# Ring slots of split weights set further apart, a bonus tied behind later chunks, and more filler ahead of the last transposes

## The chip, the cores and the metric

One core of a Trainium2 chip runs one program. The metric is the device time of one execution in microseconds (us), lower is better. TensorE (PE) has a weight loader that works beside it (PEld in the rows); VectorE is DVE, ScalarE is ACT, GpSimd is POOL, and SyncE is SP. SP and POOL issue nearly all of the DMAs.

## The reference

One layer over x of 256 tokens by 2048, in float32: an FFN, two token mixers side by side (latent attention and an RWKV recurrence) that two gates join, cross-attention into 256 memory tokens, and a second FFN. Each has an RMSNorm ahead and behind. The change sits around the recurrence and what is done to its output:

```python
def step(state, inp):                       # 16 heads, state 64 x 64 each, 256 tokens
    r_t, w_t, k_t, v_t, a_t, b_t = inp
    sa = einsum('bhvk,bhk->bhv', state, a_t)
    state = state * w_t + sa[..., None] * b_t[:, :, None, :] + v_t[..., None] * k_t[:, :, None, :]
    return state, einsum('bhvk,bhk->bhv', state, r_t)
...
o = (o - mean) * rsqrt(var + LNX_EPS)       # group norm per head
o = o * lnx_w + lnx_b
bonus = sum(rh * kh * r_k) * vh
return ((o + bonus) * g) @ w_ob             # g = sigmoid(dg) @ w_g2
```

## The kernel before

**Weights.** Every large product is done in two halves of each weight. A tile of 128 x 1024 float32 weights arrives by an SP DMA in `wraw` (4 buffers); ACT casts it to `whi` (L204) and DVE subtracts to get the rest, `wlo` (L205). Both halves go to one of RING = 3 slots of two long tiles, `whi` and `wlo`; slot s starts at WT * s = 1024 s numbers, plus a small shift (STILL) where the weights are the stationary operand. `lin_ch` (L226, L229) keeps the weights stationary, `lin_tok` (L253 to L255) streams them, three matmuls of 512 columns for each step of k and token half.

**Order of the work.** A scheduler sets the order on each engine from priorities and from readiness. In the recurrence's stage PE's order is written by hand: `weave` runs `rwkv()`, and wherever that yields a number of microseconds it puts in so many steps of `fill()`, each counted as TOK_US = 0.68. In the stretch looked at here a step of filler is three matmuls of a gate's projection (`mm<-whi,hT`), and the filler is finite: what is used early is missing later.

**The recurrence** (`rw_chain`) goes over 8 chunks of 32 tokens, numbered c0 to c7 here. In each chunk PE does `po<-S` (L953, not in c0), three steps of filler, `pu` (L963), four steps, `pn` (L972, not in c7), the rest of `po` (L982), and the first part of the next chunk's `po` (L938), then three steps. Between them ACT copies `rhs`, ACT and DVE copy one half each of `pu` into `uv` (L966), DVE makes the new state S (L979, L980; L977 in c0), and ACT copies `po` to `o`, which POOL's queue writes to memory (`osc`, L992). `last_o` counts the chunks written.

**The output** of a token half t is made of `ab` and `z`. `rw_scale` loads two rows (`lnx`) and v (`ab`) by POOL's queue, scales v by the bonus (L1010), adds a row (L1011), multiplies by the gate `pg`, a PE product (L1013, then L1014, L1015). `rw_group_norm` loads `osc` as `ov`, normalizes it on DVE with a power on POOL (L1033) and joins it with `ab` (L1035, L1036). `transposed` turns `ov` by PE (L333) into `z`, which the product with w_ob needs. For t = 0, `ab` is made early in the chain and the transposes of z[0] stand after c6; for t = 1, `ab` is tied behind the `osc` write of c6 (the argument `behind`), the group norm stands after c7, and the transposes of z[1] after 16.0 us of filler.

`after(a, b)` ties a behind b: in order alone where both are on one engine, with a semaphore otherwise.

Of the kernel before, what the change touches and what calls it, by code (L numbers as in the profile page):

```python
# [10 lines left out]
F32 = mybir.dt.float32  # L11
F32R = mybir.dt.float32r
# [6 lines left out]
P = 128  # L19
D = 2048  # L20
T = 256
# [5 lines left out]
WT = 1024  # L27
RING = 3
STILL = (64, 32)
SKEW = 4  # L30
# [49 lines left out]
class Layer:  # L80
    def __init__(self, ctx, tc, a):
# [30 lines left out]
        self.hold = []  # L112
        self.whi = self.hi_pool.tile([P, RING * WT + STILL[0]], F32R, tag="whi", name="whi")
        self.pad(self.hi_pool, 512 - 4 * STILL[0])
        self.wlo = self.lo_pool.tile([P, RING * WT + STILL[1]], F32R, tag="wlo", name="wlo")
        self.X = self.hpool.tile([P, NT, D], F32, tag="big", name="X")

    def pad(self, pool, n):

        pool.tile([P, n // 4], F32, tag="pad", name="pad")  # L120

# [63 lines left out]
    def weights(self, w, nk, c0, n, feed=None, still=False):  # L185
# [3 lines left out]
        for k in range(0, nk, kt):  # L189
            m = min(kt, nk - k)  # L190
            raw = self.wraw.tile([P, WT], F32, tag="wraw", name="wraw")
            a, b = (WT * self.turn + x for x in (STILL if still else (0, 0)))
            self.turn = (self.turn + 1) % RING
# [246 lines left out]
    def ffn(self, normed, wg, wu, wd, post):  # L440
        nc = self.nc
        h, _, row, *feed = normed
        with self.tc.tile_pool(name="hid", bufs=1) as hid:
            mh = hid.tile([P, KF, T], F32R, tag="mh", name="mh")
            ml = hid.tile([P, KF, T], F32R, tag="ml", name="ml")
            for c0 in range(0, DFF, 256):
# [3 lines left out]
                def ev_gate(j, ps):  # L450
                    sg = hid.tile([P, T], F32, tag="sg", name="sg", bufs=4)
                    nc.vector.tensor_mul(sg, ps, row())
                    nc.scalar.activation(out=sg, in_=sg, func=AF.Silu)
                    nc.vector.tensor_mul(sg, sg, row())
                    gate[j] = sg
# [88 lines left out]
    def mla_latents(self, mp, pool, normed):  # L544
        nc, w_in = self.nc, self.a["w_in"]
        h, r, _ = normed
        self.pad(pool, 224)
        self.cqh = pool.tile([P, 4, T], F32R, name="cqh")
# [192 lines left out]
    def rw_alloc(self, pool):  # L741
        self.pad(pool, 32)
        self.ar = pool.tile([P, 2, NC, GP, 64], F32, tag="ar", name="ar")
        self.bk = pool.tile([P, 2, NC, GP, 64], F32, tag="bk", name="bk")
        self.wc = pool.tile([P, NC, PAIRS], F32, tag="wc", name="wc")
        self.osc = self.dram.tile([T, 1024], F32, name="osc")
# [178 lines left out]
    def rw_chain(self, pool, G):  # L925
# [18 lines left out]
        po = from_values(0, uvs[0])  # L944
        yield 58.0
        for c in range(NC):
# [21 lines left out]
            if c < NC - 1:  # L968
# [7 lines left out]
                if S is None:  # L976
                    nc.vector.tensor_mul(Sn, pn, w)  # L977
                else:
                    nc.vector.tensor_add(Sn, S, pn)  # L979
                    nc.vector.tensor_mul(Sn, Sn, w)  # L980
            for p, h in heads:
# [4 lines left out]
            if c < NC - 1:  # L986
                S = Sn
                po = from_values(c + 1, uvs[c + 1])
            o = pool.tile([P, PAIRS, 64], F32, tag="o", name="o", bufs=2)
            nc.scalar.copy(out=o, in_=done)  # L990
# [7 lines left out]
    def rw_scale(self, pool, t, h, bon, behind):  # L998
# [10 lines left out]
        v = ab[:, 1, :].rearrange("p (h v) -> p h v", v=64)  # L1009
        nc.vector.tensor_mul(v, v, bon[:, t, h * H : (h + 1) * H].unsqueeze(2).broadcast_to([P, H, 64]))  # L1010
        nc.vector.tensor_add(ab[:, 1, :], ab[:, 1, :], rows[:, 1, :])  # L1011
        pg = self.psm.tile([P, 512], F32, tag="mm", name="pg")
        self.after(nc.tensor.matmul(pg, self.sg[:, ts], self.wg2[:, cs], start=True, stop=True), behind)  # L1013
        nc.vector.tensor_mul(ab[:, 0, :], rows[:, 0, :], pg)  # L1014
        nc.vector.tensor_mul(ab[:, 1, :], ab[:, 1, :], pg)  # L1015
# [51 lines left out]
    def mix(self, normed, xsp, stop=None):  # L1067
# [3 lines left out]
        with tc.tile_pool(name="mixp", bufs=1) as mp:  # L1071
            self.cst = mp.tile([P, NCST], F32, name="cst")
            nc.scalar.dma_start(out=self.cst, in_=a["cst"])
            self.pad(mp, 256)
            with tc.tile_pool(name="mla", bufs=1) as pool:
                self.rope_tables(pool)
                self.rw_columns(mp)
                self.mla_latents(mp, pool, normed)
                self.rw_proj_lora(mp, normed)
                self.rw_proj_v(mp, pool, normed)  # L1080
                self.mla_heads(pool)
                self.mla_attend(pool)
                rk = self.rw_proj_rk(mp, normed, 0)
# [4 lines left out]
            with tc.tile_pool(name="rwkv", bufs=1) as pool:  # L1088
# [28 lines left out]
                def rwkv():  # L1117
# [25 lines left out]
                    for i, want in enumerate(chain):  # L1143
                        if i == 4:
                            for h in range(2):
                                ab[0, h] = low(self.rw_scale, pool, 0, h, bon, self.inverted)
                        if len(self.last_o) == 4 and (0, 0) not in z:
                            for h in range(2):
                                z[0, h] = low(self.rw_group_norm, pool, 0, h, ab[0, h])
                        if len(self.last_o) == 7 and (1, 0) not in ab:  # L1150
                            low(z_tiles, mp, "r", "k")
                            for h in range(2):
                                low(self.transposed, z[0, h], zh, zl, None, 0, 4 * h)
                            for h in range(2):
                                ab[1, h] = low(self.rw_scale, pool, 1, h, bon, self.last_o[6])
                        yield want
# [3 lines left out]
                    z_tiles(pool, "ar", "bk")  # L1160
                    yield 16.0
                    for h in range(2):
                        self.transposed(z[1, h], zh, zl, None, 1, 4 * h)
                        yield 3.0

# [211 lines left out]
```

## Time and profile before

| | |
|---|---|
| median of 3 runs | 2395.17 us (2394.07 to 2395.55) |
| profiled execution, its own time | 2390.8 us |
| its span, first to last instruction | 2389.0 us |
| mean granted TensorE clock | 0.991 |
| PE busy, share of the span | 97% |
| DVE, ACT, POOL busy | 61%, 48%, 3% |
| HBM traffic | 188 GB/s over the span |

A busy PE is not a PE at its peak, since matmuls are pipelined and their ends are modelled. The pace of matmuls is therefore read as a count over a stretch of time, and lost time as that by which a stretch is longer than another with the same work.

### The profile page before, as it was taken

To read this page: it belongs to the slowest core of one execution; us is meant where nothing else is said; L and a number is where in the kernel's file an instruction comes from. 1 tells how busy PE (TensorE), PEld (TensorE's weight loads), DVE (VectorE), ACT (ScalarE), POOL (GpSimd) and SP (SyncE) were. 2 spreads that over 40 slices of the span, in tenths; PEclk is the share of its full clock that TensorE was granted. 3 is DMA by queue.
4 is the path that set the end of the run, shared out by engine and by line. 5 is a ranking of instruction groups with operands and counts; after the bars stand their busy time and mean duration, and the time that the engine had idled before them with its cause. 6 is when DMAs were issued, how large, how long until landed. Compare 5 with 4: busy or idle time off the path is not lost.

```text
span 2389.0 us, 34892 instructions
## 1 busy us (share of the span) xinstructions
PE 2329.1 (97%) x13610; PEld 1985.9 (83%) x13610; DVE 1454.2 (61%) x2117; ACT 1141.2 (48%) x1687; POOL 74.8 (3%) x128
## 2 busy tenths in 40 slices
PE   8999999999999999999998999999999999999997
PEld 7888888888887787888777788987888888888886
DVE  6666666654446576768465757556666666664444
ACT  6544445444446466534234546445544444544343
POOL 0000000000000100000121000000000000000000
PEclk9999999999999999999999999999999999999999
DMA  7555555556565654445656765544555555556654
GB/s 257 191 188 193 187 193 187 193 193 195 198 194 193 209 187 142 158 146 182 180 158 204 261 211 200 180 159 154 190 192 188 192 188 192 188 200 195 199 193 144
DMA packets 138821, 451.35 MB, mean 189 GB/s; under 512 B 24224, under 2 KB 26656, under 8 KB 138400
## 3 DMA queue, kind: packets, MB, share of 16 engines
q1 hardware_dynamic: 132992, 434.17, 54.5%
q0 software_dynamic: 4944, 14.69, 2.0%
q8 instruction: 106, 1.74, 0.3%
q10 hardware_dynamic: 720, 0.27, 0.1%
q14 instruction: 59, 0.48, 0.1%
HBM read 438.58 MB, written 10.49 MB: 188 GB/s over the span
## 4 chain that ended last, share of the span: by engine, by line
PE 49%; DVE 4%; DMA 2%; issue 1%; ACT 0%; POOL 0%; SPq 0%; DVEq 0%; POOLq 0%; ACTq 0%
PE mm L226 15%; PE mm L229 8%; PE mm L253 8%; PE mm L254 7%; PE mm L255 7%; DVE wlo L205 1%; DVE X L435 0%; DVE TT L907 0%; PE po L982 0%; DMA wraw<-in_memT 0%; PE gr L869 0%; PE pn L972 0%; PE po L953 0%; PE bt L873 0%; DVE tm L904 0%
## 5 line engine op out<-in xcount | busy, mean ns | idle before, releaser
L205 DVE TENSOR_TENSOR wlo<-wraw,whi 128x1024 fp32r<-128x1024 f32 (+2 forms) x796 | 958.4, 1207 | 731.2 <-ACT whi L204 718.7
L204 ACT CAST whi<-wraw 128x1024 fp32r<-128x1024 f32 (+2 forms) x796 | 824.1, 1036 | 889.2 <-PE mm L255 474.5
L226 PE MATMUL mm<-hT,whi 128*128 128x512 f32 x3296 | 1148.6, 394 | 6.5 <-DVE hT L324 5.3
L229 PE MATMUL mm<-hT,wlo 128*128 128x256 f32 x3296 | 913.0, 282 | 2.4 <-DVE wlo L205 2.4
L226 PEld LDWEIGHTS mm<-hT,whi 128*128 128x128 f32 x3296 | 614.1, 188 | 134.9 <-ACT whi L204 6.8
L229 PEld LDWEIGHTS mm<-hT,wlo 128*128 128x128 f32 x3296 | 621.5, 189 | 13.6 <-DVE wlo L205 4.9
L253 PE MATMUL mm<-whi,mh 128*128 128x512 f32 x688 | 267.6, 389 | 1.2 <-ACT whi L204 1.2
L254 PE MATMUL mm<-wlo,mh 128*128 128x512 f32 x688 | 267.8, 389 | 0.5 <-DVE wlo L205 0.5
L255 PE MATMUL mm<-whi,ml 128*128 128x512 f32 x688 | 267.7, 389 | 0.0
L253 PE MATMUL mm<-whi,hT 128*128 128x512 f32 (+2 forms) x512 | 190.4, 373 | 2.4 <-ACT whi L204 1.5
L254 PE MATMUL mm<-wlo,hT 128*128 128x512 f32 (+2 forms) x512 | 186.1, 364 | 5.2 <-DVE wlo L205 5.1
L255 PE MATMUL mm<-whi,hT 128*128 128x512 f32 (+2 forms) x512 | 184.7, 361 | 0.0
L253 PEld LDWEIGHTS mm<-whi,mh 128*128 128x128 f32 x688 | 129.0, 188 | 28.4 <-ACT whi L204 1.5
L254 PEld LDWEIGHTS mm<-wlo,mh 128*128 128x128 f32 x688 | 129.1, 188 | 27.8 <-DVE wlo L205 1.0
L255 PEld LDWEIGHTS mm<-whi,ml 128*128 128x128 f32 x688 | 129.1, 188 | 26.6
L235 ACT COPY half<-mm 128x256 f32<-128x256 f32 x206 | 75.1, 366 | 136.7 <-PE mm L226 136.7
L236 DVE TENSOR_TENSOR half<-half,mm 128x256 f32<-128x256 f32 x206 | 85.8, 418 | 54.6 <-ACT half L235 54.6
L254 PEld LDWEIGHTS mm<-wlo,hT 128*128 128x128 f32 x512 | 97.7, 191 | 21.8 <-DVE wlo L205 8.3
L253 PEld LDWEIGHTS mm<-whi,hT 128*128 128x128 f32 x512 | 97.5, 191 | 19.7 <-ACT whi L204 2.2
L255 PEld LDWEIGHTS mm<-whi,hT 128*128 128x128 f32 x512 | 97.4, 190 | 14.4
L288 POOL TENSOR_TENSOR rstd<-rstd,mhalf 128x1 f32<-128x1 f32 x22 | 12.1, 553 | 1811.5 <-DVE rstd L286 1811.5
L253 PE MATMUL mm<-whi,oT 128*128 128x512 f32 x128 | 50.8, 397 | 2.3 <-ACT whi L204 2.3
(278 smaller groups left out, 1733.3 us busy)
## 6 DMA issues: line engine op xcount, KB each, us to landing
wraw<-in_w_ffn_up SPq DMA_DIRECT2D x172, 512.0 KB, 3.4
wraw<-in_w_ffn_gate SPq DMA_DIRECT2D x171, 512.0 KB, 3.5
wraw<-in_w_ffn_down SPq DMA_DIRECT2D x168, 512.0 KB, 4.2
wraw<-in_w_in SPq DMA_DIRECT2D x124, 512.0 KB, 3.5
wraw<-in_w_o SPq DMA_DIRECT2D x32, 512.0 KB, 4.3
wraw<-in_w_ckv SPq DMA_DIRECT2D x31, 512.0 KB, 3.5
wraw<-in_w_oa SPq DMA_DIRECT2D x16, 512.0 KB, 3.9
wraw<-in_w_ob SPq DMA_DIRECT2D x16, 512.0 KB, 4.1
```

The costliest lines, as they stand in the source:

```text
L204: cast = nc.scalar.copy(out=hi[:, e], in_=raw[:, e])
L205: self.last_split = nc.vector.tensor_sub(out=lo[:, e], in0=raw[:, e], in1=hi[:, e].bitcast(F32))
L226: both = lambda: nc.tensor.matmul(ps[j], hi[:, s], x[:, k], start=(k == 0), stop=(k == nk - 1))
L229: nc.tensor.matmul(ps[j][:, 0, :], lo[:, s], x[:, k, 0], start=False, stop=False)
L235: nc.scalar.copy(out=y, in_=ps[j][:, 1, :])
L236: nc.vector.tensor_add(y, y, ps[j][:, 0, :])
L253: nc.tensor.matmul(ps[t], part(xh, t, k), hi, start=(k == 0), stop=False)
L254: nc.tensor.matmul(ps[t], part(xh, t, k), lo, start=False, stop=False)
L255: self.last_mm = nc.tensor.matmul(ps[t], part(xl, t, k), hi, start=False, stop=(k == nk - 1))
L288: nc.gpsimd.tensor_tensor(out=r, in0=r, in1=self.mhalf, op=ALU.pow)
```

## The change

The slots of the ring lie SLOT = WT + 128 = 1152 numbers apart in place of 1024. The bytes for it come from two `sg` buffers of the FFN and one `o` buffer of the chain; the pads are set anew, and each size of pad now has a tag of its own. `ab` of t = 0 is built when two chunks are written, in place of at the fifth stop of the chain, and its bonus multiply and its first gate multiply are tied behind the latest S update on DVE (`last_S`). The transposes of z[0] stand one chunk earlier, `ab` of t = 1 is tied behind `last_o[5]` in place of `last_o[6]`, and `pg` is tied behind nothing. One more step of filler stands ahead of c0's `pu`; 26.0 us in place of 16.0 ahead of the last transposes, and 5.0 in place of 3.0 after each.

```diff
+SLOT = WT + 128
...
-        self.whi = self.hi_pool.tile([P, RING * WT + STILL[0]], F32R, tag="whi", name="whi")
+        self.whi = self.hi_pool.tile([P, (RING - 1) * SLOT + WT + STILL[0]], F32R, tag="whi", name="whi")
...
-        pool.tile([P, n // 4], F32, tag="pad", name="pad")
+        pool.tile([P, n // 4], F32, tag=f"pad{n}", name="pad")
...
-            a, b = (WT * self.turn + x for x in (STILL if still else (0, 0)))
+            a, b = (SLOT * self.turn + x for x in (STILL if still else (0, 0)))
...
-                    sg = hid.tile([P, T], F32, tag="sg", name="sg", bufs=4)
+                    sg = hid.tile([P, T], F32, tag="sg", name="sg", bufs=2)
...
-        yield 58.0
+        yield 59.0
...
-                    nc.vector.tensor_mul(Sn, Sn, w)
+                    self.last_S = nc.vector.tensor_mul(Sn, Sn, w)
...
-            o = pool.tile([P, PAIRS, 64], F32, tag="o", name="o", bufs=2)
+            o = pool.tile([P, PAIRS, 64], F32, tag="o", name="o", bufs=1)
...
-        nc.vector.tensor_mul(v, v, bon[:, t, h * H : (h + 1) * H].unsqueeze(2).broadcast_to([P, H, 64]))
+        scaled = nc.vector.tensor_mul(v, v, bon[:, t, h * H : (h + 1) * H].unsqueeze(2).broadcast_to([P, H, 64]))
+        self.after(scaled, self.last_S)
         nc.vector.tensor_add(ab[:, 1, :], ab[:, 1, :], rows[:, 1, :])
         pg = self.psm.tile([P, 512], F32, tag="mm", name="pg")
-        self.after(nc.tensor.matmul(pg, self.sg[:, ts], self.wg2[:, cs], start=True, stop=True), behind)
-        nc.vector.tensor_mul(ab[:, 0, :], rows[:, 0, :], pg)
+        nc.tensor.matmul(pg, self.sg[:, ts], self.wg2[:, cs], start=True, stop=True)
+        self.after(nc.vector.tensor_mul(ab[:, 0, :], rows[:, 0, :], pg), self.last_S)
...
-                        if i == 4:
+                        if len(self.last_o) == 2 and (0, 0) not in ab:
                             for h in range(2):
                                 ab[0, h] = low(self.rw_scale, pool, 0, h, bon, self.inverted)
...
-                        if len(self.last_o) == 7 and (1, 0) not in ab:
+                        if len(self.last_o) == 6 and not zh:
                             low(z_tiles, mp, "r", "k")
                             for h in range(2):
                                 low(self.transposed, z[0, h], zh, zl, None, 0, 4 * h)
+                        if len(self.last_o) == 7 and (1, 0) not in ab:
                             for h in range(2):
-                                ab[1, h] = low(self.rw_scale, pool, 1, h, bon, self.last_o[6])
+                                ab[1, h] = low(self.rw_scale, pool, 1, h, bon, self.last_o[5])
...
-                    yield 16.0
+                    yield 26.0
                     for h in range(2):
                         self.transposed(z[1, h], zh, zl, None, 1, 4 * h)
-                        yield 3.0
+                        yield 5.0
```

**Three places in the order.** Line numbers of the changed kernel are one to four higher. First, DVE in c0 and c1 before the change: `ab` is the bonus product of t = 0, `uv` the copy that PE's `pn` needs, S the state.

```order
L205 TENSOR_TENSOR wlo<-wraw,whi 128x1024 x4
L1010 TENSOR_TENSOR ab<-ab,bon 128x512
L1011 TENSOR_TENSOR ab<-ab,lnx 128x512
L205 TENSOR_TENSOR wlo<-wraw,whi 128x1024
L966 COPY uv<-pu 32x512
L1010 TENSOR_TENSOR ab<-ab,bon 128x512
L1011 TENSOR_TENSOR ab<-ab,lnx 128x512
L977 TENSOR_TENSOR S<-pn,wc 128x512
```

In the changed kernel DVE has this in c0, and the second S update of c1 is followed by the rows of the fence after it.

```order
L206 TENSOR_TENSOR wlo<-wraw,whi 128x1024 x5
L967 COPY uv<-pu 32x512
L978 TENSOR_TENSOR S<-pn,wc 128x512
L206 TENSOR_TENSOR wlo<-wraw,whi 128x1024
L1050 SCALAR_TENSOR_TENSOR gt<-mm,rstd,g 128x512
```

```order
L981 TENSOR_TENSOR S<-S,wc 128x512
L1011 TENSOR_TENSOR ab<-ab,bon 128x512
L1016 TENSOR_TENSOR ab<-lnx,pg 128x512
L1013 TENSOR_TENSOR ab<-ab,lnx 128x512
L1011 TENSOR_TENSOR ab<-ab,bon 128x512
L1017 TENSOR_TENSOR ab<-ab,pg 128x512
L1013 TENSOR_TENSOR ab<-ab,lnx 128x512
L1016 TENSOR_TENSOR ab<-lnx,pg 128x512
L1017 TENSOR_TENSOR ab<-ab,pg 128x512
L206 TENSOR_TENSOR wlo<-wraw,whi 128x1024
L967 COPY uv<-pu 32x512
```

The four multiplies and adds that stood around c0's copy are gone from there, and all eight operations on `ab` stand in one block behind c1's state; c2's `uv` copy comes after the block and one split. At the end of c6 DVE has the same eight with two splits among and behind them ahead of c7's copy.

Second, PE at the end of c6 before the change (`tr<-ident,ov` are the transposes of z[0], `pg` the gate product of t = 1):

```order
L972 MATMUL pn<-uv,bk 64x64 x16
L982 MATMUL po<-uv,G 32x64 x16
L938 MATMUL po<-uv,G 64x64 x16
L333 MATMUL tr<-ident,ov 128x128 x8
L1013 MATMUL pg<-wg_9184,sg 128x512 x2
L253 MATMUL mm<-whi,hT 128x512
```

In the changed kernel PE has the transposes at the end of c5, and `pg` alone at the end of c6:

```order
L939 MATMUL po<-uv,G 64x64 x16
L334 MATMUL tr<-ident,ov 128x128 x8
L254 MATMUL mm<-whi,hT 128x512
L255 MATMUL mm<-wlo,hT 128x512
L256 MATMUL mm<-whi,hT 128x512
```

```order
L983 MATMUL po<-uv,G 32x64 x16
L939 MATMUL po<-uv,G 64x64 x16
L1015 MATMUL pg<-wg_9185,sg 128x512 x2
L254 MATMUL mm<-whi,hT 128x512
L255 MATMUL mm<-wlo,hT 128x512
```

The transposes moved one chunk ahead, and `pg` of t = 0 likewise stands at the end of c1 where it stood behind c1's `pu`. After c7's `po` PE had 24 steps of filler, 4 transposes, 5 steps, 4 transposes and 36 steps; it now has 39, 4, 8, 4 and 17. Ahead of c0's `pu` 86 steps became 87.

Third, ACT at the end of the first FFN's gate and up products before the change (`sg` is the gate, `mh` its product with the up half):

```order
L321 CAST mh<-sg 128x256
L235 COPY half<-mm 128x256
L453 ACTIVATE sg<-sg 128x256
L204 CAST whi<-wraw 128x1024 x3
L235 COPY half<-mm 128x256
L321 CAST mh<-sg 128x256
L204 CAST whi<-wraw 128x1024 x18
```

In the changed kernel ACT has there:

```order
L322 CAST mh<-sg 128x256
L205 CAST whi<-wraw 128x1024
L236 COPY half<-mm 128x256
L205 CAST whi<-wraw 128x1024
L454 ACTIVATE sg<-sg 128x256
L205 CAST whi<-wraw 128x1024
L236 COPY half<-mm 128x256
L205 CAST whi<-wraw 128x1024
L322 CAST mh<-sg 128x256
L205 CAST whi<-wraw 128x1024 x17
```

The casts of the next weights now stand between the evictions in place of behind them, one of them ahead of the first. Smaller moves of this kind stand in the latent attention and in the cross-attention, where the transposes ahead of the first query stand later among the products of keys and values.

## Rows read from the trace of the kernel before

**Rows 1.** The page: busy time by engine, and the split on DVE.

```profile
PE 2329.1 (97%) x13610; PEld 1985.9 (83%) x13610; DVE 1454.2 (61%) x2117; ACT 1141.2 (48%) x1687; POOL 74.8 (3%) x128
...
L205 DVE TENSOR_TENSOR wlo<-wraw,whi 128x1024 fp32r<-128x1024 f32 (+2 forms) x796 | 958.4, 1207 | 731.2 <-ACT whi L204 718.7
```

**Rows 2.** Waits of PE, 1140 to 1290 us: total, times, longest.

```profile
PE tr L333 <- DVE ov L1036: 7.4, 1, 7.4
PE pn L972 <- DVE uv L966: 5.0, 1, 5.0
PE pg L1013 <- DMA osc<-o: 2.5, 1, 2.5
```

**Rows 3.** Windows: length, busy PE, PEld, DVE, ACT, POOL (x), PEclk, DMA, GB/s.

```profile
1143.67:1175.74 32.07, 26.28 (x335) 20.63 (x334) 15.86 (x21) 7.47 (x11) 4.04 (x9) 0.84 0.66 206
1188.54:1201.33 12.79, 12.79 (x194) 10.27 (x190) 4.53 (x6) 3.85 (x5) 1.95 (x5) 1.00 0.41 135
1194.21:1201.33 7.12, 7.12 (x141) 6.03 (x140) 3.29 (x4) 2.21 (x3) 0.47 (x1) 1.00 0.46 144
1188.54:1198.16 9.62, 9.62 (x98) 7.33 (x94) 2.78 (x4) 3.26 (x4) 1.49 (x4) 1.00 0.38 128
1199.24:1200.26 1.02, 1.02 (x37) 0.93 (x33) 0.86 (x2) 0.00 (x0) 0.00 (x0) 1.00 0.60 116
1167.14:1168.56 1.42, 1.42 (x9) 0.70 (x5) 1.39 (x2) 0.97 (x2) 0.00 (x0) 1.00 0.00 0
1287.38:1287.73 0.35, 0.35 (x6) 0.35 (x4) 0.00 (x0) 0.16 (x1) 0.00 (x0) 1.00 0.00 0
1239.71:1257.32 17.61, 15.07 (x142) 10.59 (x138) 10.24 (x15) 4.33 (x6) 4.11 (x8) 0.90 0.55 155
1257.32:1287.73 30.41, 22.78 (x100) 18.01 (x96) 17.83 (x26) 10.80 (x14) 8.66 (x12) 0.89 0.63 204
1085.00:1143.60 58.60, 58.60 (x260) 48.31 (x258) 51.67 (x96) 26.39 (x29) 2.12 (x4) 1.00 0.62 198
```

**Rows 4.** Timeline of POOL and of DVE in c0: start, length, line, idle before.

```profile
1143.15 0.54 POOL L1008 DMA_DIRECT2D ab<-vsh  x1
...
1150.19 0.69 DVE L1010 TENSOR_TENSOR ab<-ab,bon 128x512 f32<-128x512 f32 x1 [7.50 <-DMA ab<-vsh]
```

**Rows 5.** Timeline of DVE and of PE in two undisturbed chunks.

```profile
1187.86 0.69 DVE L980 TENSOR_TENSOR S<-S,wc 128x512 f32<-128x512 f32 x1
...
1198.16 0.74 PE L972 MATMUL pn<-uv,bk 64*64 64x64 f32 x18
```

**Rows 6.** Timeline of DVE: the ends of the group norms of t = 0 and t = 1.

```profile
1225.39 0.69 DVE L1036 TENSOR_TENSOR ov<-ov,ab 128x512 f32<-128x512 f32 x1
...
1281.31 1.29 DVE L1036 TENSOR_TENSOR ov<-ov,ab 128x512 f32<-128x512 f32 x2
```

**Rows 7.** Timeline of POOL: the group norm's power, both heads of t = 0.

```profile
1216.16 1.66 POOL L1033 TENSOR_TENSOR gv<-gv,mhalf 128x8 f32<-128x8 f32 x1
1220.83 2.06 POOL L1033 TENSOR_TENSOR gv<-gv,mhalf 128x8 f32<-128x8 f32 x1 [3.01 <-DVE gv L1032]
```

**Rows 8.** DMA issues: size and median us to landing.

```profile
osc<-o POOLq DMA_DIRECT2D x16, 64.0 KB, 2.6
```

**Rows 9.** Waits of PE, 480 to 500 us, the end of the first FFN's gates.

```profile
PE mm L253 <- ACT whi L204: 1.2, 1, 1.2
PE mm L254 <- DVE wlo L205: 0.5, 1, 0.5
```

**Rows 10.** Waits of PE, 1440 to 1510 us, the cross-attention's start: the longest.

```profile
PE mm L254 <- DVE wlo L205: 1.5, 2, 1.0
```

**Rows 11.** Windows: first FFN's gates, its down product, product with w_ob.

```profile
100.00:400.00 300.00, 300.00 (x1733) 264.13 (x1732) 194.26 (x271) 147.20 (x216) 0.00 (x0) 1.00 0.56 190
...
500.00:640.00 140.00, 140.00 (x619) 115.95 (x618) 64.92 (x57) 57.08 (x61) 0.00 (x0) 1.00 0.60 196
...
1313.00:1326.00 13.00, 13.00 (x57) 10.52 (x57) 8.16 (x9) 5.86 (x7) 1.08 (x2) 1.00 0.75 239
```

More of the change, by code (lines that the diff above doesn't have):

```diff
@@ L112, in __init__ @@
         self.hold = []
-        self.whi = self.hi_pool.tile([P, RING * WT + STILL[0]], F32R, tag="whi", name="whi")
+        self.whi = self.hi_pool.tile([P, (RING - 1) * SLOT + WT + STILL[0]], F32R, tag="whi", name="whi")
         self.pad(self.hi_pool, 512 - 4 * STILL[0])
-        self.wlo = self.lo_pool.tile([P, RING * WT + STILL[1]], F32R, tag="wlo", name="wlo")
+        self.wlo = self.lo_pool.tile([P, (RING - 1) * SLOT + WT + STILL[1]], F32R, tag="wlo", name="wlo")
         self.X = self.hpool.tile([P, NT, D], F32, tag="big", name="X")
     def pad(self, pool, n):
-        pool.tile([P, n // 4], F32, tag="pad", name="pad")
+        pool.tile([P, n // 4], F32, tag=f"pad{n}", name="pad")
     def col(self, name, j):
@@ L546, in mla_latents @@
         h, r, _ = normed
-        self.pad(pool, 224)
+        self.pad(pool, 64)
         self.cqh = pool.tile([P, 4, T], F32R, name="cqh")
@@ L741, in rw_alloc @@
     def rw_alloc(self, pool):
-        self.pad(pool, 32)
+        self.pad(pool, 384)
         self.ar = pool.tile([P, 2, NC, GP, 64], F32, tag="ar", name="ar")
@@ L1073, in mix @@
             nc.scalar.dma_start(out=self.cst, in_=a["cst"])
-            self.pad(mp, 256)
+            self.pad(mp, 96)
             with tc.tile_pool(name="mla", bufs=1) as pool:
@@ L1080, in mix @@
                 self.rw_proj_v(mp, pool, normed)
+                self.pad(mp, 320)
                 self.mla_heads(pool)
```

## The prediction

> **What bounds the kernel now.** The page comes first: PE is busy for 97% of the span [rows 1], so time can come from two places alone, PE's waits and the pace of its matmuls. The waits of PE around the chain come second: in the 150 us from 1140 on there are three long ones, 7.4, 5.0 and 2.5 us [rows 2], each once. They are too short to explain the stretch, so windows over it come third. An undisturbed chunk takes 12.79 us with PE busy throughout and the clock at 1.00 [rows 3]; I had the same length for each of c2 to c6. Against it I set the stretches that hold the waits.
>
> - c0 and c1, from c0's `pu`: 32.07 us. The same work undisturbed is the tail of a chunk from `pu` on, 7.12, a whole chunk, 12.79, and one `pg`, 1.42, together 21.33. Lost: 10.74.
> - c7 with what stands ahead of it: 17.61 us. Undisturbed: eight transposes, 2 x 0.35, `pg`, 1.42, a chunk up to `pn`, 9.62, and the rest of `po`, 1.02, together 12.76. Lost: 4.85.
> - From c7's end to the last transposes: 30.41 us for 24 + 5 steps of filler, 87 matmuls, and two times four transposes. The pace of filler is 58.60 us for 260 matmuls, 0.2254 each, so 19.61 + 0.70 = 20.31. Lost: 10.10 (all [rows 3]).
>
> That is 25.69 us, of which the waits are 14.9. The rest is mostly the clock: 0.84, 0.90 and 0.89 in these windows. With levels of 2.4 and 1.2 GHz that is 32%, 20% and 22% of their time at 1.2, some 20 us, and 20 us at half pace are 10 us of work. In each window the clock fell behind the wait; the undisturbed chunks, with the same small matmuls, hold 1.00 [rows 3].
>
> **The change, part by part.**
>
> *The bonus behind c1's state.* `ab` was issued at 1143.15 and DVE waited for it until 1150.19, with the `uv` copy queued behind [rows 4]; PE's `pn` waited 5.0 us for that copy [rows 2]. In the new order the copy follows the splits directly and `ab` is first touched one and a half chunks later, when it has long landed. The 10.74 of c0 and c1 go. What is new is a block of eight operations of 0.69 us on DVE behind S of c1, 5.5 us, then one split, 1.21 [rows 1], then the copy for c2, 0.7: 7.4 us behind S. PE asks for the copy at `pn`: in the undisturbed chunks S ends at 1188.55 and `pn` starts at 1198.16, 9.61 us later [rows 5], and `pg` adds 1.42. So it is hidden, with 2.2 us or more to spare. The splits held up by the block feed 12 matmuls each; a chunk uses 30 of those in 12.79 us, 2.5 tiles, and three slots stand filled. Were that cover gone, each us beyond costs PE one.
>
> *`pg` without its tie, transposes one chunk earlier.* The 2.5 us wait of `pg` for c6's `osc` write [rows 2] has no cause left, and the loads of `lnx` and `ab` for t = 1 go out behind c5's write, a chunk (12.79 us) ahead of their use, so DVE no longer stands still for them. The 4.85 of c7 go. What is late next is z[0]: its group norm ends at 1225.39 + 0.69 = 1226.08 [rows 6], and PE reaches the end of c5 at 1226.92, two undisturbed chunks behind 1201.33 [rows 3]. The margin is 0.8 us; one split of 1.2 us more ahead of it eats it. Between 0 and 1.2 I take a cost of 1.0, once.
> The block of eight at c6 has two splits ahead of c7's copy: 8.7 us against 9.61 + 1.42, hidden.
>
> *More filler.* 39 steps in place of 24 stand ahead of the last transposes: 117 x 0.2254 = 26.4 us behind c7's `po`. The group norm of t = 1 ended at 1281.31 + 1.29 = 1282.60 [rows 6], 25.3 us behind it (1257.32, where the window of [rows 3] begins), both heads; the new order finishes the first head ahead of the second. The 7.4 us wait and the slow clock behind it, 10.10, go. The filler is not lost: 65 steps before, 64 now and one in c0. The 17 left at the end, 11.5 us, cover the splitting of z[1].
>
> A rule speaks against this margin. The power on POOL took 1.66 us with DVE idle and 2.06 where DVE ran beside it [rows 7]: 0.4 more, for two heads 0.8, less than the 1.1 between 25.3 and 26.4. The Trainium skill, "SBUF — State Buffer", section "Who interferes with whom", says that a DVE instruction with two SBUF inputs and a GpSimd one that reads SBUF exclude each other for the whole instruction; the new order puts such a split behind each variance. By that rule each power could wait for a split, 2.4 us for two, and the last transposes would wait 1.3, which makes the sum 25.1 in place of 26.4; the row showed 0.4, and I stay with it.
>
> *Single `o`, two `sg`.* `o` is written once in 12.79 us, and its write lands 2.6 us after issue [rows 8]; this is hidden, and from a landing of about 11 us on ACT would stand still in each chunk. `sg` is a pair per block of gates, and the next block's gates end a whole product later. Both 0.
>
> *The first FFN's end.* The casts for the down weights stood behind evictions that wait for PE; PE then waited 1.2 and 0.5 us [rows 9]. The new order is that of the second FFN's end, where PE's list of waits is empty. 1.7 us go; bounds 0 and 1.7.
>
> *The cross-attention's start* is reordered without a wait that I can place. Its longest wait in total is 1.5 us [rows 10]. I take 0, bounds 1.5 either way.
>
> *The slots.* No operation is added, and nothing here shows slots at this distance. The pace is 300.00 / 1733 = 0.1731 us a matmul in the gates (512 and 256 columns by turns) and 140.00 / 619 = 0.2262 in the down product, and 13.00 / 57 = 0.2281 with w_ob, whose z lies at odd places [rows 11]. One matmul more or less in 619 is 0.16%, 4 us of the span: I take 0, bounds 4 either way from this, and the 0.8% of w_ob for the rival below.
>
> **Sum.** 10.74 + 4.85 + 10.10 + 1.7 - 1.0 = 26.4 us, from the profiled execution's 2390.8 to 2364.4. The median of the runs lies 4.4 above that execution, so 2369.
>
> **The rivals.**
>
> 1. *The waits move to the copies.* The blocks of eight hold DVE longer than counted, because a split in them waits for its cast; `pn` of c2 and `po` of c7 wait in turn. Two waits of 3 us with 1.5 us of slow clock each: 9 us back, 2378. For it: DVE's order is fixed, and splits wait for casts. Against: 2.2 us spare.
> 2. *The last transposes still wait.* Only 1.1 us of margin by the old end of the group norm. Late by 4 us with 2 of slow clock: 2375. For it: the chain runs over POOL and DVE by turns. Against: the first head now ends ahead of the second.
> 3. *The clock stays low.* If the small matmuls and not the waits made it fall, only the waits and little else go: 10 us fewer, 2379. Against: 1.00 in the undisturbed chunks.
> 4. *Slower.* Reads of weights at the new places slow PE everywhere. At 1.5% of 2329 us busy [rows 1] it costs 35: 2404. It decides from (26.4 + 4.8) / 2329 = 1.3% on. For it: a pace that differs by 0.8% with z. Against: that is the largest departure, and it lies below 1.3%.
>
> **How the numbers follow.** The forecast 0.66, with a range of its own of 2364 to 2374. Rival 1 has 0.12, rival 2 0.10, rival 3 0.05, rival 4 0.04; 0.03 for what I don't see. Downwards the bounds of the slots, the cross-attention and the 1.0 add to 6.5, rarely all: 2360 takes in the most. Upwards rivals 1 to 3, with 4 more for the slots: 2385. Some 0.2 us in 100, 4.8 us, is about what a measurement of this kernel can tell from no change. Faster by more: the forecast and rivals 1 to 3, 0.93. Within: 0.03. Slower: 0.04.
>
> **What would show it.** In the profile after, the three rows of PE's waits [rows 2] are gone; all chunks of the chain have 12.79 us, with 1.42 more where `pg` stands and 0.7 with the transposes; the clock is 1.00 from c0 to the product with w_ob; DVE waits for no `ab` or `lnx`; ACT casts without a wait of PE at the end of the first FFN; and the matmuls of both FFNs keep 0.1731 and 0.2262 us. A wait of `pn` for `uv` in c2, one of the transposes at c5, or a changed pace in the FFNs would make me wrong, the last by the most.

## The result, and the profile after

The changed kernel takes 2367.1 us in the median of 4 runs (2363.9 to 2374.3), the kernel before 2394.6 in runs beside it (2393.4 to 2395.6): 0.989 of the time, 95% interval 0.9864 to 0.9915, or 27.5 us less. The execution whose profile follows is the slowest of the four, 2374.3 us with a span of 2372.2, so what is lost in its rows is more than what the median holds.

The page, busy PE, against [rows 1]:

```profile
PE 2326.5 (98%) x13610; PEld 1987.4 (84%) x13610; DVE 1453.2 (61%) x2117; ACT 1142.4 (48%) x1687; POOL 77.9 (3%) x128
```

Waits of PE, 1130 to 1310 us, against [rows 2]: total, times, longest.

```profile
PE mm L255 <- DVE wlo L206: 3.6, 3, 1.4
PE pn L973 <- DVE uv L967: 3.2, 2, 2.8
PE po L939 <- issue: 2.0, 1, 2.0
PE pu L964 <- DMA G<-td: 0.2, 1, 0.2
```

The three waits of before are gone: no `tr`, no `pg`, and the `pn` that is left is another one, in c5. New are splits that come late, and 2.0 us in c0 "issue", which is a wait for nothing that the profile names. What these do to the stretches is in the windows, against [rows 3]: c0 and c1 with `pg`; an undisturbed chunk; c5 with the transposes of z[0]; c7 with `pg`; from c7's end to the last transposes.

```profile
1137.40:1164.13 26.73, 24.53 (x336) 19.25 (x335) 12.18 (x15) 7.95 (x11) 4.91 (x10) 0.87 0.81 253
1177.17:1189.97 12.80, 12.80 (x195) 10.27 (x191) 5.06 (x6) 4.85 (x6) 1.97 (x5) 1.00 0.39 129
1203.50:1222.26 18.76, 15.97 (x203) 13.21 (x199) 13.42 (x22) 6.32 (x9) 8.82 (x11) 0.88 0.52 169
1236.07:1248.38 12.31, 12.31 (x134) 9.01 (x130) 8.82 (x13) 4.12 (x5) 1.01 (x2) 1.00 0.33 110
1248.38:1279.53 31.15, 27.58 (x121) 21.79 (x118) 19.45 (x27) 12.52 (x17) 10.20 (x13) 1.00 0.66 201
```

With the lengths of undisturbed work from the prediction: c0 and c1 still lose 26.73 - 21.33 = 5.4 us, c5 loses 18.76 - 12.79 - 0.70 = 5.3, which it did not before, c7 loses nothing to speak of, and 31.15 us stand where 26.4 were counted, with the clock at 1.00: 4.7 lost, 3.6 of it in the three waits for splits. Of the 25.7 us that these stretches lost before, this execution loses 15.4 again, so the stage gained some 10 us where 24.7 were expected. The two profiled spans differ by 16.8 us (2389.0 and 2372.2), so some 6 must have come from elsewhere, and the experiments say from where.

What makes c5 wait stands in DVE's timeline there: start, length, line, in brackets the idle time before.

```profile
1206.69 1.22 DVE L206 TENSOR_TENSOR wlo<-wraw,whi 128x1024 fp32r<-128x1024 f32 x1
...
1211.39 0.69 DVE L1038 TENSOR_TENSOR ov<-ov,ab 128x512 f32<-128x512 f32 x1
1213.61 0.69 DVE L1036 TENSOR_TENSOR ov<-ov,gv 128x512 f32<-128x512 f32 x1 [1.53 <-POOL gv L1035]
1214.22 1.22 DVE L206 TENSOR_TENSOR wlo<-wraw,whi 128x1024 fp32r<-128x1024 f32 x1
1215.47 0.69 DVE L967 COPY uv<-pu 32x512 f32<-32x512 f32 x1
```

The copy for c5's `pn` stands behind a multiply of the group norm of t = 0, which waits 1.53 us for POOL's power, and behind a split. PE does two matmuls of `pn` at 1213.10 and waits for the copy with the rest:

```profile
1213.10 0.33 PE L973 MATMUL pn<-uv,bk 64*64 64x64 f32 x2
1216.21 1.14 PE L973 MATMUL pn<-uv,bk 64*64 64x64 f32 x30 [2.79 <-DVE uv L967]
```

In the kernel before, DVE has c5's copy ahead of that multiply:

```profile
1221.43 0.69 DVE L966 COPY uv<-pu 32x512 f32<-32x512 f32 x1
1222.92 0.69 DVE L1034 TENSOR_TENSOR ov<-ov,gv 128x512 f32<-128x512 f32 x1 [0.81 <-POOL gv L1033]
```

The pace of the FFNs, against [rows 11], is what it was, 1733 and 619 matmuls:

```profile
100.00:400.00 300.00, 300.00 (x1733) 264.18 (x1732) 194.13 (x271) 147.48 (x217) 0.00 (x0) 1.00 0.58 190
500.00:640.00 140.00, 140.00 (x619) 115.91 (x619) 65.48 (x57) 56.28 (x61) 0.00 (x0) 1.00 0.63 197
```

### The profile page after: what moved, and what is told of

Same layout as the page of the kernel before. It is cut to its first block, busy times and chain, and to the rows that moved or that the text cites. A ratio compares the mean times of both kernels' runs of the same rounds, so it can differ in the third digit from the quotient of the medians.

```text
span 2372.2 us, 34910 instructions
## 1 busy us (share of the span) xinstructions
PE 2326.5 (98%) x13610; PEld 1987.4 (84%) x13610; DVE 1453.2 (61%) x2117; ACT 1142.4 (48%) x1687; POOL 77.9 (3%) x128
## 4 chain that ended last, share of the span: by engine, by line
PE 49%; DVE 4%; DMA 2%; issue 1%; POOL 1%; ACT 0%; SPq 0%; DVEq 0%; POOLq 0%; ACTq 0%
PE mm L227 16%; PE mm L230 8%; PE mm L254 7%; PE mm L255 7%; PE mm L256 7%; DVE wlo L206 1%; DVE TT L908 0%; POOL gv L1035 0%; PE gr L870 0%; DVE X L436 0%; PE tr L361 0%; PE bt L874 0%; DVE tm L905 0%; PE xo L1260 0%; PE xsc L1249 0%
## 5 line engine op out<-in xcount | busy, mean ns | idle before, releaser
L230 PEld LDWEIGHTS mm<-hT,wlo 128*128 128x128 f32 x3296 | 621.8, 189 | 12.5 <-DVE wlo L206 3.7
```

What stands on the lines that cost most here:

```text
L230: nc.tensor.matmul(ps[j][:, 0, :], lo[:, s], x[:, k, 0], start=False, stop=False)
```

## The experiments

Three sets of runs, each beside runs of the kernel before (medians 2394.4, 2395.0 and 2394.7).

### The parts alone

**The slots, with their buffers and pads**, and of the recurrence's stage nothing but the single `o`:

```diff
+SLOT = WT + 128
...
-            a, b = (WT * self.turn + x for x in (STILL if still else (0, 0)))
+            a, b = (SLOT * self.turn + x for x in (STILL if still else (0, 0)))
...
-                    sg = hid.tile([P, T], F32, tag="sg", name="sg", bufs=4)
+                    sg = hid.tile([P, T], F32, tag="sg", name="sg", bufs=2)
```

> The kernel before with the wider slots, the two sg and one o buffers and the pads alone; the recurrence's stage keeps its order. This brings the new order at the end of the first FFN, in the latent attention and at the start of the cross-attention with it. Theory A, slots cost nothing, only those orders count: the matmuls of both FFNs keep 0.1731 and 0.2262 us, the two waits at the first FFN's end are gone (1.7 us), and other waits in the two attentions change by a few us: 2389 to 2393, against 2394.6 before. Theory B, the distance of the slots changes PE's pace: the pace rows differ from 0.1731 and 0.2262, and the time leaves 2389 to 2393, downwards if reads get faster, above 2395 if slower.

Measured: 2384.6 us, 0.9961 [0.9949, 0.9973], 9.8 us faster. Neither theory has it: the pace is the same (1733 and 619 matmuls in the two windows), and the time is below the range of theory A. The slots are worth far more than the 1.7 us counted for the first FFN's end, and not by the pace.

**The changed kernel without the slots:**

```diff
-SLOT = WT + 128
...
-            a, b = (SLOT * self.turn + x for x in (STILL if still else (0, 0)))
+            a, b = (WT * self.turn + x for x in (STILL if still else (0, 0)))
...
```

> The changed kernel without the slots, buffers and pads: bonus tied behind S, pg untied, transposes of z[0] one chunk earlier, more filler. Theory A, the prediction's terms of the recurrence's stage hold: 10.74 + 4.85 + 10.10 - 1.0 = 24.7 us faster than before, 2370, with 3 more or less. Rival 1, the waits move to the copies of uv and to the splits: PE waits for uv in c5 and for wlo after c7 as in the profile of the changed kernel, and those are there in every execution: 2378 or more. If the slots mattered (theory B of the run above), the two runs do not add up to the whole change's 27.

Measured: 2379.3 us, 0.994 [0.9928, 0.9952], 15.1 us faster and not 24.7. Rival 1 holds, with rows that repeat those of the changed kernel (waits of PE, 1130 to 1310 us):

```profile
PE pn L972 <- DVE uv L966: 3.1, 2, 2.8
PE mm L254 <- DVE wlo L205: 2.9, 3, 1.2
```

**The bonus alone:**

```diff
-                    nc.vector.tensor_mul(Sn, Sn, w)
+                    self.last_S = nc.vector.tensor_mul(Sn, Sn, w)
...
+        self.after(scaled, self.last_S)
...
-                        if i == 4:
+                        if len(self.last_o) == 2 and (0, 0) not in ab:
```

> The kernel before with the bonus alone: ab of t = 0 built when two chunks are written, its first multiply and first gate multiply behind the latest S. Theory A: the waits of pn and the slow clock in c0 and c1 go, 10.7 us, 2384; no wait of pn for uv in c2. Rival 1: the block of eight on DVE makes pn of c2 wait, 3 us and 1.5 of slow clock: 2388. Third, as the profile of the changed kernel has it: a wait of 2 us in c0 for nothing shown, with the slow clock behind it, takes 5 us of the gain, 2389.

Measured: 2383.1 us, 0.9961 [0.9949, 0.9973], 11.3 us faster; theory A. The chain's `pn` has no row any more, and the window over c0 and c1, from `pu` on, is 22.95 us at a clock of 1.00 where it was 32.07 at 0.84:

```profile
1145.55:1168.50 22.95, 21.83 (x335) 17.23 (x335) 11.30 (x14) 6.88 (x11) 6.06 (x13) 1.00 0.92 288
```

The block of eight on DVE makes nobody wait in c2.

**`pg` and the transposes alone:**

```diff
-        self.after(nc.tensor.matmul(pg, self.sg[:, ts], self.wg2[:, cs], start=True, stop=True), behind)
+        nc.tensor.matmul(pg, self.sg[:, ts], self.wg2[:, cs], start=True, stop=True)
...
-                        if len(self.last_o) == 7 and (1, 0) not in ab:
+                        if len(self.last_o) == 6 and not zh:
...
+                        if len(self.last_o) == 7 and (1, 0) not in ab:
...
-                                ab[1, h] = low(self.rw_scale, pool, 1, h, bon, self.last_o[6])
+                                ab[1, h] = low(self.rw_scale, pool, 1, h, bon, self.last_o[5])
```

> The kernel before with pg untied, the transposes of z[0] one chunk earlier and the loads of t = 1 behind c5's write, alone. Theory A, the prediction's terms: 4.85 of c7 less up to 1.0 for z[0] at c5: 3.85, 2390.7. Rival: the group norm of t = 1 or z[0] at c5 takes it back in new waits: 2394.5, with a row of tr for ov at c5 or a longer one at the last transposes than 7.4.

Measured: 2390.6 us, 0.9983 [0.9974, 0.9992], 4.1 us faster; theory A. The row of `pg` is gone, and `tr` has the one it had, 7.4, at the last transposes; none at c5.

**The filler alone:**

```diff
-        yield 58.0
+        yield 59.0
...
-                    yield 16.0
+                    yield 26.0
...
-                        yield 3.0
+                        yield 5.0
```

> The kernel before with the filler alone: 59 in place of 58 ahead of c0, 26.0 in place of 16.0 us ahead of the last transposes, 5.0 in place of 3.0 behind each four. Theory A: the wait of tr, 7.4 us, and the slow clock behind it go, 10.1 us: 2384.5. Rival 2: the transposes still wait, 2389, with a row of PE's waits for ov. Third: the filler waits for splits that stand behind the group norm on DVE, 4.6 us as in the profile of the changed kernel, at full clock: 2389, with rows of PE's waits for wlo.

Measured: 2395.0 us, 1.0002 [0.9994, 1.0011]: nothing. The wait of `tr` is gone as theory A has it, but `pn` now waits 10.0 us in place of 5.0, 7.2 of it in c0 and 2.8 in c5 (waits of PE, 1130 to 1310 us):

```profile
PE pn L972 <- DVE uv L966: 10.0, 2, 7.2
...
PE mm L254 <- DVE wlo L205: 1.8, 2, 0.9
```

None of the three theories named this. The row of 2.8 is that of the changed kernel, in a kernel that shares only the filler with it. Of the filler, one step stands ahead of both places.

**The filler without the step ahead of c0**, 58.0 as before, 26.7 ahead of the last transposes:

```diff
-                    yield 16.0
+                    yield 26.7
...
-                        yield 3.0
+                        yield 5.0
```

> The kernel before with 26.7 in place of 16.0 us of filler ahead of the last transposes and 5.0 in place of 3.0 behind each four, but 58.0 ahead of c0 as it was. Theory A: the filler's term of 10.1 is there when the step ahead of c0 is left alone, less what filler waits for splits behind the group norm (2.5 to 4.6 us in the profiles with this filler): 2387 to 2389, and no wait of pn for uv in c5. Rival: this filler brings nothing with 58 either, 2394.

Measured: 2386.5 us, 0.9972 [0.996, 0.9983], 8.2 us faster; theory A. `pn` has its one wait of c0, and the filler behind c7 waits for splits:

```profile
PE pn L972 <- DVE uv L966: 5.7, 1, 5.7
PE mm L254 <- DVE wlo L205: 4.2, 3, 2.0
```

### What the slots do

**The changed kernel once more:**

> The changed kernel once more, with a second profile. Theory A: the stalls in c0 (2 us for nothing shown) and in c5 (pn for uv, 3 us) each bring a stretch of slow clock; the one in c5 stands in every execution since DVE's order is fixed, the one in c0 only in some, which would explain a spread of 2364 to 2374. Then a profile without the stall in c0 has 5 us less, 2366 to 2370, and the median stays at 2367. Rival: the stall in c0 is in each profile and the spread comes from elsewhere.

Measured: 2367.6 us (2363.9 to 2368.0), 0.9881 [0.9867, 0.9894]. In this profile, too, c0 has its wait for nothing shown (1.8 us) and c5 its 2.8. The spread is not settled by it.

**The changed kernel with slots 1024 apart again**, the bytes in pads:

```diff
-SLOT = WT + 128
+SLOT = WT
...
-        self.pad(self.hi_pool, 512 - 4 * STILL[0])
+        self.pad(self.hi_pool, 1536 - 4 * STILL[0])
...
+        self.pad(self.lo_pool, 1024)
```

> The changed kernel with slots 1024 numbers apart again and everything else at its place (the two sg and one o buffers stay; the bytes go to pads). Theory A: with 1024 a stationary tile, which is shifted by 64 or 32 numbers, reaches into the next slot, so the first cast for a streamed product waits until the last matmul of a stationary one; the waits at the end of the first FFN's gates (2.3 us), in the latent attention, and at 963 and 1014 us come back, in the sum about 10 us: 2377. Rival: the buffers made the orders, not the slots: no change, 2367.

Measured: 2380.1 us, 0.9935 [0.9923, 0.9948], 12.5 us slower than the changed kernel beside it; between the two profiled spans it is 2374.9 - 2366.1 = 8.8. Theory A. The waits of PE for casts and splits over the whole span, first with 1024:

```profile
PE mm L256 <- DVE wlo L207: 8.6, 12, 1.2
...
PE mm L255 <- ACT whi L206: 5.4, 6, 1.2
...
PE mm L231 <- DVE wlo L207: 2.8, 5, 0.7
...
PE mm L228 <- ACT whi L206: 0.6, 1, 0.6
```

and in the changed kernel of the same set:

```profile
PE mm L255 <- DVE wlo L206: 5.6, 6, 1.8
...
PE mm L230 <- DVE wlo L206: 1.9, 3, 0.9
...
PE mm L227 <- ACT whi L205: 1.2, 1, 1.2
...
PE mm L254 <- ACT whi L205: 0.2, 1, 0.2
```

17.4 against 8.9 us, 8.5 of the 8.8 between the spans. (Between the medians it is more because the profiled execution with 1024 is the fastest of its five.) How one of them comes about is to be seen at the end of the first FFN's gates. ACT's timeline with 1024:

```profile
488.43 1.05 ACT L206 CAST whi<-wraw 128x1024 fp32r<-128x1024 f32 x1 [0.86 <-PE mm L228]
491.36 2.00 ACT L206 CAST whi<-wraw 128x1024 fp32r<-128x1024 f32 x2 [1.89 <-PE mm L228]
```

PE there, the last matmul with stationary weights and the first with streamed ones:

```profile
490.88 0.40 PE L228 MATMUL mm<-hT,whi 128*128 128x512 f32 x1
492.46 0.73 PE L255 MATMUL mm<-whi,mh 128*128 128x512 f32 x2 [1.18 <-ACT whi L206]
```

The cast at 491.36 starts when the gates' last matmul is through, and PE then waits for the cast; the one at 488.43 is for the streamed tile after that, whose slot was free. A stationary tile is shifted by 64 numbers in `whi` and 32 in `wlo`, so with 1024 it ends inside the next slot; the next streamed tile begins at that slot's start, and its cast must wait for the last reader of the tile ahead of it, not for that of the tile three turns ago. One slot of the three is lost for a moment where a streamed product follows a stationary one, unless the last stationary tile lies in the third slot, behind which no slot begins. The order of the tiles in the kernel puts the last stationary one of the first FFN, the 172nd of all, into the first slot, and that of the second FFN, the 702nd, into the third. So the second FFN's end is the counter-example at the same distance of 1024: in the kernel before, the cast for the first streamed tile runs 5 us ahead there, and PE's first streamed matmul has no wait (timeline of ACT and PE):

```profile
2136.48 1.05 ACT L204 CAST whi<-wraw 128x1024 fp32r<-128x1024 f32 x1 [1.54 <-issue]
...
2141.79 0.39 PE L253 MATMUL mm<-whi,mh 128*128 128x512 f32 x1
```

With 1152 the casts run ahead (ACT, the changed kernel):

```profile
487.49 1.05 ACT L205 CAST whi<-wraw 128x1024 fp32r<-128x1024 f32 x1 [1.53 <-issue]
...
490.15 1.05 ACT L205 CAST whi<-wraw 128x1024 fp32r<-128x1024 f32 x1 [1.34 <-issue]
```

**Slots 1088 apart**, where nothing overlaps either:

```diff
-SLOT = WT + 128
+SLOT = WT + 64
...
-        self.pad(self.hi_pool, 512 - 4 * STILL[0])
+        self.pad(self.hi_pool, 1024 - 4 * STILL[0])
...
+        self.pad(self.lo_pool, 512)
```

> The changed kernel with slots 1088 numbers apart, 64 more than before and 64 fewer than in the changed kernel; pads keep everything else at its place and all orders are the same. Theory A, the gain of the slots (8.8 us between two profiled executions, 12.5 between medians) is that a shifted stationary tile no longer reaches into the next slot: with 64 it doesn't either, so 2367 as the changed kernel, the two rows of waits at the end of the first FFN absent. Rival, the distance counts by itself: between 2367 and 2380, or the pace rows of the FFNs move from 0.1731 and 0.2262.

Measured: 2368.4 us, 0.989 [0.9877, 0.9904], as the changed kernel. It is the overlap, not the distance.

### The step of filler, and the loads in c0

**One step of filler back behind the chain:**

```diff
-        yield 59.0
+        yield 58.0
...
-                    yield 26.0
+                    yield 26.7
```

> The changed kernel with 58.0 in place of 59.0 us of filler ahead of c0's pu and 26.7 in place of 26.0 ahead of the last transposes: one step of filler moves from there to here. Theory A: the extra step ahead of c0 has put a multiply of the group norm, which waits for POOL's power, and a split ahead of c5's copy of uv on DVE; without it the wait of pn in c5 (3 us) and the slow clock behind it (3 us) go: 2361, with no row of pn for uv over 0.7 us. Rival: the group norm holds DVE in c5 either way, the wait stays: 2367.

Measured: 2361.9 us, 0.9858 [0.9843, 0.9874], 5.7 us less than the changed kernel beside it; theory A. DVE in c5 has the copy ahead of the multiply that waits for POOL:

```profile
1207.14 0.69 DVE L1038 TENSOR_TENSOR ov<-ov,ab 128x512 f32<-128x512 f32 x1
1207.87 0.69 DVE L967 COPY uv<-pu 32x512 f32<-32x512 f32 x1
1209.36 0.69 DVE L1036 TENSOR_TENSOR ov<-ov,gv 128x512 f32<-128x512 f32 x1 [0.81 <-POOL gv L1035]
```

and c5 with the transposes is 13.65 us where it was 18.76:

```profile
1200.56:1214.21 13.65, 13.65 (x203) 11.13 (x199) 10.93 (x18) 4.97 (x8) 6.63 (x8) 1.00 0.51 169
```

**The same with the loads of `lnx` and `ab` for t = 0 behind c0's write:**

```diff
-                                ab[0, h] = low(self.rw_scale, pool, 0, h, bon, self.inverted)
+                                ab[0, h] = low(self.rw_scale, pool, 0, h, bon, self.last_o[0])
```

> The kernel of the run before with the six loads of lnx and ab for t = 0 tied behind c0's write in place of behind the inverse, so that they no longer stand with the loads of G and of weights between 1135 and 1146 us, where the DMA engines are busy throughout. Theory A: the waits of c0 (0.2 for G, 2 us for nothing shown) come from that crowd and go, with the slow clock behind them: 2 to 5 us less than the run before in the median, 2357 to 2360, and a narrower spread. Rival: they have another cause: the same as the run before. DVE, PE and ACT keep their order.

Measured: 2360.5 us, 0.9855 [0.9842, 0.9868]. It is the fastest of all here, but not distinguishable from the run before: the rival.

**The changed kernel with these loads moved**, the line of the last diff and nothing else:

> The changed kernel, with 59.0 and 26.0 as it has them, but the six loads of lnx and ab for t = 0 tied behind c0's write. PE, DVE and ACT keep their order. Theory A: the 1.8 to 2.0 us in c0 for which the profile shows no cause (in both profiles of the changed kernel) come with the crowd of loads; they go, and with them the 6.8 us of slow clock at 1145: 2362 to 2364. Rival: they come from something else, 2367 and the row of po for nothing shown stays.

Measured: 2366.4 us, 0.9879 [0.9864, 0.9894]. The row of `po` for nothing shown is absent, but it is absent with 1088 too, whose loads were not moved, and the median is that of the changed kernel. So theory A is not borne out: the wait comes in some executions. c0's timeline in the changed kernel shows that it falls between matmuls of one kind, after 20 of 32:

```profile
1143.92 0.80 PE L939 MATMUL po<-uv,G 32*64 32x64 f32 x20
1146.71 0.91 PE L939 MATMUL po<-uv,G 32*64 32x64 f32 x12 [1.99 <-issue]
```

With slots 1024 apart (1.0 us) it falls after 20 as well. With 58.0 (0.7 us) three matmuls fewer stand ahead of c0, and it falls after 23, so it keeps its place in PE's stream of instructions:

```profile
1146.52 0.50 PE L939 MATMUL po<-uv,G 32*64 32x64 f32 x9 [0.67 <-issue]
```

The profile has a DMA queue for instructions, too, with one packet from 1143 to 1150 us in the changed kernel (packets, MB, share of 16 engines):

```profile
q8 instruction: 1, 0.02, 1.0%
```

It starts at 1144.24. In all four profiles with this wait PE goes on 2.3 to 2.5 us behind the start of such a packet; with 1088 and with the loads moved in the changed kernel PE comes to the place 2.7 and 4.7 us behind it, and does not wait. So the wait is most likely one for instructions that come late. No run moved such a packet alone, so this is argued and not shown.

## Why the prediction's total was right and two of its steps were not

The time came out 2 us below the forecast, inside its own range, but by luck: in the sum two errors cancel, 7.6 us too much counted for the filler and 8.1 too little for the slots. Of the signs that were named, the three rows of waits and the pace came as said; the lengths of c0, c1 and c5 and the clock there did not. By terms, each against the median of before in its own set, in us gained:

| term | predicted | measured |
|---|---|---|
| bonus behind c1's state | 10.7 | 11.3 (alone) |
| `pg` and transposes, less 1.0 at c5 | 3.85 | 4.1 (alone) |
| filler ahead of the last transposes | 10.1 | 8.2 (alone, 58.0) |
| the step ahead of c0 | 0 | -5.7 (taken out of the changed kernel) |
| slots, first FFN's end, cross-attention | 1.7 | 9.8 (alone), 12.5 (taken out) |
| sum | 26.4 | 27.7 with 9.8 |

27.7 stands against 27.5 measured for the whole. Each measured term is uncertain by 2 to 4 us, and by the ratios in place of the medians the bonus has 9.3, the filler 6.7, and the sum is 23.9 against 26.3, so the closeness of 27.7 to 27.5 says little; the stage without the slots gave 15.1, 2.8 short of its four terms' 17.9.

- **The bonus** went as worked out, the 2.2 us of slack behind the block of eight included (in the changed kernel c2's copy ends at 1171.88 and its `pn` starts at 1174.01), and the slow clock went with the wait: with the bonus alone it is 1.00 over c0 and c1, where only short waits for `G` were left. That the small matmuls and not the waits pull the clock down (rival 3) is out.
- **c7 and z[0].** No transposes waited at c5; the margin of 0.8 us that I feared for was the right place and the wrong instruction. What is late at c5 is the `uv` copy.
- **"65 steps before, 64 now and one in c0": costed at nothing, and this is the first step that failed.** I counted filler as work that moves without loss. The step shifts the stream of splits against the chain by three matmuls, the order on DVE is set anew with it, and at c5 a multiply that waits for POOL and a split fall ahead of the copy: 5.7 us, of which the wait is 2.8. It is rival 1's kind of loss at a place that rival 1 did not name: not the blocks of eight in c2 and c7, which the margins covered, but the group norm of t = 0. The order on DVE at c5 in both kernels would have shown it: the copy stands ahead of that multiply before, and behind it after.
- **The last transposes** do not wait, as forecast. The term is 2 us smaller because DVE's splits stand between the group norm's operations and wait with them: filler that covers a chain on DVE is itself fed by DVE. I counted the 117 matmuls at their undisturbed pace. In the changed kernel the longest of PE's three waits there, 1.4 us, ends with a split that stands behind the group norm's wait for its load:

```profile
1261.26 0.69 DVE L1029 TENSOR_REDUCE gm<-ov 128x8 f32<-128x512 f32 x1 [3.39 <-DMA ov<-osc]
...
1262.67 1.22 DVE L206 TENSOR_TENSOR wlo<-wraw,whi 128x1024 fp32r<-128x1024 f32 x1
```

- **"The slots. No operation is added": 0, bounds 4 either way, by pace alone. This is the second step that failed.** The pace is indeed the same. What I did not ask is what a tile's place makes wait: the shift of the stationary tiles and the distance of 1024 were both in sight, and 1024 + 64 reaches into the next slot. The new order of casts at the first FFN's end, which I took for the whole gain (1.7 us), was the visible end of it: the cast there waited for the overlap and not only for its place behind the evictions. Such waits stood at other places, too, where a streamed product follows a stationary one, but not at the second FFN's end, where the shift reaches into no slot; that the two ends differ was in sight. Rival 4, slower by pace, is out.
- **The rule weighed against the power's row** holds in kind, and the row came nearer in size. POOL's timeline in the changed kernel has the power of t = 0 twice, and last the second one of t = 1:

```profile
1206.87 2.57 POOL L1035 TENSOR_TENSOR gv<-gv,mhalf 128x8 f32<-128x8 f32 x1 [1.67 <-DVE gv L1034]
...
1211.52 2.06 POOL L1035 TENSOR_TENSOR gv<-gv,mhalf 128x8 f32<-128x8 f32 x1 [2.08 <-DVE gv L1034]
...
1272.40 1.81 POOL L1035 TENSOR_TENSOR gv<-gv,mhalf 128x8 f32<-128x8 f32 x1
```

The split at 1206.69 (DVE's timeline above) ran 1.22, so 1.04 us of it lay behind the power's start; the power took 0.91 more than the 1.66 with DVE idle [rows 7]. The second began at 1211.52, with 0.56 of L1038 left (the row at 1211.39 above), and took 0.40 more. That is nearly the rest of the DVE instruction each time, as the Trainium skill, "SBUF — State Buffer", section "Who interferes with whom", has it: one shared port pair, locked by one of the two. The 0.4 that I took from [rows 7] was not the size of the effect but what was left of one instruction. For the heads of t = 1, which the weighing was about, splits had 1.04 and 0.28 us left when the powers started (the second split from 1271.46 on), and the powers took 0.91 and 0.15 more: 1.1 us together, nearer to the 0.8 of the row than to the 2.4 that I drew from the rule, since the splits had begun ahead of the powers. The last transposes were not late by it: the first head ends at 1271.48, 3.3 us ahead of the 1274.8 that the forecast gives them, and PE came 4.7 us later still.

## What to carry to other kernels

When tiles of one ring are placed with a shift, check that shifted and unshifted tiles share no number: an overlap of 64 in 1024 cost 9 to 12 us here, in waits that each look like an engine being late, and the pace shows nothing. Filler moved past a chain is not free even if none is lost: read the order of the engine that feeds the filler at each step of the chain behind it, and what stands ahead of the chain's copies there. A total that fits is no evidence for its terms; one run for each term is.

## What was not expected of the hardware

PE waited 1.8 to 2.0 us amid 32 like matmuls, for nothing that the profile names, in both profiles of the changed kernel, 1.0 with 1024 and 0.7 with 58.0, each time until 2.3 to 2.5 us behind the start of a packet of instructions; with 1088 and with the loads moved this was absent from c0. With 1088 a wait of this kind, 1.8 us, stood ahead of a matmul of `lora` at 936 us, with no such packet starting between 915 and 940 us; its cause stays open. Around the one in c0 DVE and ACT were idle too, POOL issued DMAs, and the DMA engines were busy throughout (busy PE 0.01, PEld, DVE and ACT 0.00, the DMA share 1.00):

```profile
1144.70:1146.70 2.00, 0.01 (x2) 0.00 (x0) 0.00 (x0) 0.00 (x0) 1.82 (x4) 0.85 1.00 242
```

The granted clock fell behind single waits of 1.8 to 2.8 us, but not behind the three waits of up to 1.4 us in the filler after c7, where it is 1.00. In the changed kernel's c0 it is 1.00 up to the wait of 2.0 us and then half, the lower of its levels of 2.4 and 1.2 GHz, before it is 1.00 again from 1153.0 on:

```profile
1146.70:1150.00 3.30, 3.29 (x18) 2.69 (x19) 0.00 (x0) 0.00 (x0) 0.00 (x0) 0.50 1.01 376
```
